# Four gate blocks in the opening of a hybrid layer, paired modulation visits, and ten early z blocks

## The chip, the cores and the metric

The kernel runs on one core of a Trainium2 chip. Its time is the device time of one execution in microseconds (us); the number given for a version is the median of its runs. The core's engines each work through their own list of instructions and meet at semaphores: PE (TensorE, matmuls; PEld is its weight loads, which overlap), DVE (VectorE), ACT (ScalarE), POOL (GpSimd) and SP (SyncE, which here issues nearly all DMA transfers). Results of PE go to banks of the PSUM memory (`pm`, `ps`), which the other engines read and free.

## The reference

One inference step of one decoder layer for a prompt of 256 tokens and 8 sequences with 8 new tokens each (320 rows), width 2048. Two branches read the same modulated input through one combined projection, and are merged by sigmoid gates:

```python
mod = silu(c) @ w_ada + b_ada                       # 9 conditioning rows (1 prompt, 8 sequences)
shift, scale, gate = split(mod, 3)
h = rms_norm(x, pre_norm_g) * (1 + scale) + shift
(a_qkv, a_z, a_b, a_a, b_q, b_k, b_v, b_z, i_q, i_k, i_w, g_a, g_b) = split_columns(h @ w_in)
y_a, s_new, conv_new = gdn_branch(...)              # short conv, gated delta rule, rms_norm(o) * silu(a_z)
y_b = attend(q, k, v, qi, i_w, i_k) * silu(b_z)     # top-k indexer, sparse attention
merged = sigmoid(g_a) * (y_a @ w_pa) + sigmoid(g_b) * (y_b @ w_pb)
return x + gate * rms_norm(merged @ w_out, post_norm_g)
```

The delta rule keeps a state S of 128 x 128 per head (32 heads, 8 sequences and the prompt) and updates it chunk by chunk: `s = s * g_tail + k_tail.T @ u`.

## The kernel before, in words

**Main products.** A product with a big weight matrix is done in float32 precision by splitting the weights (`whi`, `wlo`) and the activations (`xh`, `xl`) in a high and a low part. The unit of work is a half block: 8 x 128 rows of the weights by 128 columns, loaded by SP into `raw` (512 KB), split by ACT (`whi`) and DVE (`wlo = raw - whi`), and multiplied on PE by 8 x 3 matmuls with all 320 rows moving (`xh,whi`, `xl,whi`, `xh,wlo`). Two halves make a block of 128 output columns. `stream()` runs through a list of such half blocks, splits two ahead, and lets the other work ("sides", Python generators such as `prompt_chain`, `sample_chain`, `gate_gen`) put its instructions between them; a planner with its own clock decides when each side may go on. When something must be complete at a point (a buffer, a group), `force` puts all that is missing there in one go. The outcome is a fixed order for each engine.

**Stages.** *Opening* (`startup`): the modulation of x. In eight visits q, 256 columns of `shift` and 256 of `scale` are computed. `w_ada` comes in tiles of 1024 x 256 (`raw`, `rawx`, 1 MB); PE takes the 9 conditioning rows (padded to 32 columns, `cT`) as weights in four column groups of 32, each group summing every fourth row block, with 256 columns moving; `columns(q, e, h)` is one tile (e: shift or scale, h: half of the rows), `operands` copies the result to `msb`, adds the four partial sums and turns the rows into columns by four small products with `sel`, and modulates two row blocks of x into `xh`, `xl`. Each visit then has the two row blocks it needs to do, for its eighth of the width, part of the products of 8 index-query blocks (`iq_job`, 256 of the 320 rows), one value block (`bv_job`) and five auxiliary blocks (`held_job`, weights `awr` split to `awh`, `awl`). Partial sums of the first two are added in SBUF by DVE. These jobs wait in a list (`jobs`), and `run(n)` takes the next n. SP loads in the order in which `seq` lists: four tiles of `w_ada`, `i` (1 MB), `w` (720 KB), next visit; a load whose buffer is not free holds up those behind it.

*Attention*: the stream of the remaining 8 index-query blocks, 16 q, 16 z of mixer B, 16 blocks of the gate g_a (`ga`, kept in DRAM as `d_siga`), and the z blocks of mixer A named in `EARLY_Z` (two per entry); beside it all of the indexer, top-k and attention, and `gate_gen`, which computes the third part of the modulation like the opening does, in eight visits. *Gdn*: eight groups of four heads, each k, q, z and v blocks; beside it the recurrences. In a recurrence, PE multiplies the state (`w`, `S`) with `kq`, DVE forms `vt`, PE multiplies `XT,vt`, DVE and ACT form new `w`, PE multiplies `w,ktok`, and DVE updates S in 16 steps (`S<-S,gtr,ps`). z blocks that attention has done are left out of their groups, so groups 0 and 1 have 20 half blocks and the others 24. *Tail*: gate g_b, the two projections and the output product.

All engine calls go through one helper, so most rows of the profile carry its line, 63 (64 in the changed kernel), and are told apart by tile names.

Of the kernel before, what the change touches and what calls it, by code (L numbers as in the profile page):

```python
# [17 lines left out]
NP = 256  # L18
# [17 lines left out]
EARLY = 8  # L36
AHEAD = 4

EARLY_Z = (0, 4)
# [165 lines left out]
class Kernel:  # L205
# [259 lines left out]
    def consts(self):  # L465
# [6 lines left out]
        self.ident_b = self.l0.tile([128, 128], BF, name="ident_b")  # L472
        v.tensor_copy(self.ident_b, self.ident)
# [19 lines left out]
    def startup(self):  # L493
# [12 lines left out]
        awl = sp.tile([128, 2, 720], F32R, name="awl")  # L506
        seq = []
        for q in range(8):
            seq += [("a", q, 0), ("a", q, 1), ("a", 8 + q, 0), ("a", 8 + q, 1), ("i", q, 0), ("w", q, 0)]
        raws, aws, iqs = {}, {}, {}  # L510
        pos = {"n": 0}

        def load():
            while pos["n"] < len(seq):
                kind, q, h = seq[pos["n"]]
                r = awr if kind == "w" else ring
# [8 lines left out]
                elif kind == "w":  # L525
                    for d0, c0, n in ((0, C_IK, 144), (144, C_BA, 64), (208, C_BK, 512)):
                        nc.sync.dma_start(t[:, :, d0:d0 + n], w[rows, c0:c0 + n].rearrange("(k p) c -> p k c", p=128))
                    aws[q] = t
                else:
# [15 lines left out]
        for e in range(2):  # L545
            nc.scalar.dma_start(x[2][64 * e:64 * e + 64], xs[:, 1024 * e:1024 * e + 1024])
# [21 lines left out]
        seli = sp.tile([128, 9, 4], I32, name="seli")  # L568
        nc.gpsimd.iota(seli, pattern=[[-1, 9], [-32, 4]], base=0, channel_multiplier=1)
        self4 = sp.tile([128, 9, 4], F32, name="self4")  # L570
        nc.vector.tensor_scalar(self4, seli, 0.0, None, op0=OP.is_equal)
        self.sel = self.l0.tile([128, 9], F32, name="sel")
        nc.vector.tensor_reduce(self.sel, self4, axis=AX.X, op=OP.add)
# [17 lines left out]
        both = sp.tile([128, 128], F32, name="both")  # L591
        for e in range(2):
            self.tt(both[:, 64 * e:64 * e + 64], self.ident[:, 0:64], self.ident[:, 64:128], OP.add)
# [23 lines left out]
        msb = sp.tile([128, 512], F32, name="msb")  # L617
# [14 lines left out]
        def split_i(q, g):  # L632
# [13 lines left out]
            low()  # L646

# [48 lines left out]

        def first_jobs():
# [8 lines left out]
        def jobs(q):  # L706
            if q == 0:
                fifo.append(first_jobs)
            for h in range(3 if q == 0 else 0, EARLY):
                fifo.append(lambda h=h: iq_job(q, h))  # L710
            fifo.append(lambda: bv_job(q))
            for j in range(len(held)):
                fifo.append(lambda j=j: held_job(q, j))
# [5 lines left out]
        def columns(q, e, h, p):  # L719
            t, whole = raws.pop((q + 8 * e, h))  # L720
            for k in range(8):
                kb, j = 8 * h + k, k % 4
                self.mm(p[32 * j:32 * j + 32, 256 * e:256 * e + 256], self.cT[:, kb, :], t[:, k, :], start=(kb < 4),
                        stop=(kb >= 12), skip=True)
            drop(t, whole)

        def operands(q, turned=None):
# [3 lines left out]
            for e in range(4):  # L731
                self.mm(p[:, 9 * e:9 * e + 9], msb[:, 128 * e:128 * e + 128], self.sel)
# [3 lines left out]
            for e, qq in enumerate((q, 8 + q)):  # L736
                self.tt(mod[:, 2 * qq:2 * qq + 2, :], p[:, 18 * e:18 * e + 18].rearrange("p (e s) -> p e s", s=9),
# [11 lines left out]
        for q in range(8):  # L749
# [12 lines left out]
            else:  # L762
                idle_turns(10)
            if q == 1:
                run(2)
                split(0)
                run(2)
            p = self.ps_main.get()
            columns(q, 0, 0, p)
            if q == 0:  # L770
                idle_turns(14)
            columns(q, 0, 1, p)
            if q == 0:
                idle_turns(14)
            elif q == 1:
                run(4)
            else:
                split(q - 1)
                run(5)
            if q >= AHEAD:  # L780
                split_i(q, 0)
            columns(q, 1, 0, p)
            if q == 0:
# [5 lines left out]
                idle_turns(8)  # L789
            columns(q, 1, 1, p)  # L790
            self.act(msb, p)
# [4 lines left out]
            elif q > 1:  # L796
                run(4)
# [11 lines left out]
        run(5)  # L809
# [1637 lines left out]
```

## Time and profile before

| | |
|---|---|
| median of 3 runs | 2132.27 us (2132.07 to 2133.04) |
| profiled execution | 2132.65 us, span 2130.9 us |
| granted clock, mean | 0.998 |
| PE, PEld, DVE, ACT, POOL busy | 99%, 94%, 66%, 46%, 22% |
| opening, until the first half block of the stream | 0 to 169.5 us |
| attention | 169.5 to 715.7 us |
| gdn | 715.7 to 1659.5 us |
| tail | to the end |

Times in rows are in us from the start of the span; "mean ns" is the duration of one instruction, which for matmuls overlaps with the next: the cost of one on PE is the distance between starts. A matmul of two float32 operands is recorded as two passes. In brackets stands idle time of the engine ahead of a row, and what ended it.

### The profile page before, as it was taken

To read this page: it belongs to the slowest core of one execution; us is meant where nothing else is said; L and a number is where in the kernel's file an instruction comes from. 1 tells how busy PE (TensorE), PEld (TensorE's weight loads), DVE (VectorE), ACT (ScalarE), POOL (GpSimd) and SP (SyncE) were. 2 spreads that over 40 slices of the span, in tenths; PEclk is the share of its full clock that TensorE was granted. 3 is DMA by queue.
4 is the path that set the end of the run, shared out by engine and by line. 5 is a ranking of instruction groups with operands and counts; after the bars stand their busy time and mean duration, and the time that the engine had idled before them with its cause. 6 is when DMAs were issued, how large, how long until landed. Compare 5 with 4: busy or idle time off the path is not lost.

```text
span 2130.9 us, 43963 instructions
## 1 busy us (share of the span) xinstructions
PE 2099.3 (99%) x17055; PEld 2006.3 (94%) x17055; DVE 1410.9 (66%) x2881; ACT 989.6 (46%) x2257; POOL 463.1 (22%) x653
## 2 busy tenths in 40 slices
PE   7999999999999999999999999999999999999997
PEld 5889999899999999999999999999999999999997
DVE  4665657899755678868787878787746545445543
ACT  3235464333344455565656565656535424233343
POOL 2000100000001036545444444445440000000000
PEclk9999999999999999999999999999999999999999
DMA  9996656985787766777877777777787967555562
GB/s 332 355 309 173 181 151 178 289 256 151 201 238 239 205 181 173 211 210 207 207 200 199 208 196 210 193 212 192 200 218 210 268 180 218 161 155 146 166 178 85
DMA packets 720336, 438.91 MB, mean 206 GB/s; under 512 B 74144, under 2 KB 705536, under 8 KB 717824
## 3 DMA queue, kind: packets, MB, share of 16 engines
q1 hardware_dynamic: 716032, 413.45, 68.9%
q0 software_dynamic: 3616, 21.02, 3.0%
q8 instruction: 134, 2.20, 0.4%
q10 hardware_dynamic: 480, 1.65, 0.3%
q14 instruction: 74, 0.61, 0.1%
HBM read 386.81 MB, written 48.94 MB: 204 GB/s over the span
## 4 chain that ended last, share of the span: by engine, by line
PE 72%; issue 23%; DMA 2%; DVE 2%; ACT 0%; SPq 0%; DVEq 0%; POOL 0%; POOLq 0%; ACTq 0%
PE pm L63 56%; PE ps L63 16%; DMA raw<-in_w_ada_dram 1%; DVE S L63 1%; DMA rawx<-in_w_in_dram 1%; DVE wlo L63 0%; SPq L63 0%; DMA c<-in_c_sample_dram 0%; DVE awl L63 0%; DMA out_dram<-S 0%; ACT whi L63 0%; ACT ot L63 0%; DVE sga L63 0%; DVE w L63 0%; DVEq L2443 0%
## 5 line engine op out<-in xcount | busy, mean ns | idle before, releaser
L63 PE MATMUL pm<-xh,whi 128*128 128x320 f32 (+1 forms) x3284 | 996.1, 317 | 1.9 <-DVE qiS L63 0.8
L63 PE MATMUL pm<-xl,whi 128*128 128x320 f32 (+1 forms) x3284 | 962.1, 307 | 0.4 <-DVE xl L63 0.3
L63 DVE TENSOR_TENSOR wlo<-raw,whi 128x1024 fp32r<-128x1024 f32 x474 | 589.1, 1252 | 280.8 <-ACT whi L63 264.9
L63 PEld LDWEIGHTS pm<-xh,whi 128*128 128x128 f32 x3284 | 617.6, 188 | 32.2 <-issue 23.9
L63 PEld LDWEIGHTS pm<-xl,whi 128*128 128x128 f32 x3284 | 618.1, 188 | 1.7 <-DVE xl L63 0.8
L63 ACT ACTIVATE whi<-raw 128x1024 fp32r<-128x1024 f32 x474 | 497.7, 1058 | 169.7 <-PE pm L63 150.8
L63 PE MATMUL pm<-xh,wlo 128*128 128x320 f32 (+1 forms) x3284 | 547.6, 307 | 0.0
L63 PEld LDWEIGHTS pm<-xh,wlo 128*128 128x128 f32 x3284 | 495.4, 188 | 0.0
L63 POOL TENSOR_TENSOR X<-X,tmpx 48x31 f32<-48x31 f32 (+15 forms) x248 | 175.9, 709 | 19.4
L63 POOL TENSOR_TENSOR tmpx<-blk,X 48x31 f32<-48x31 f32 (+15 forms) x248 | 160.4, 647 | 51.0 <-DMA blk<-d_b 32.8
L63 PE MATMUL pm<-y1h,whi 128*128 128x320 f32 x512 | 151.3, 308 | 1.1 <-ACT y1h L63 1.1
L63 PE MATMUL pm<-y1l,whi 128*128 128x320 f32 x512 | 151.3, 307 | 0.2
L63 DVE SCALAR_TENSOR_TENSOR ps<-xp,cs,ps 128x344 f32<-128x344 f32 x192 | 111.5, 581 | 6.8
L63 POOL TENSOR_TENSOR rfin<-rfin,mh 128x3 f32<-128x3 f32 x1 | 0.8, 848 | 486.4 <-DVE rfin L63 486.4
L63 POOL TENSOR_TENSOR sc<-sc,mh 128x6 f32<-128x6 f32 (+1 forms) x24 | 43.6, 1815 | 277.0 <-DVE sc L63 213.0
L63 PEld LDWEIGHTS pm<-y1h,whi 128*128 128x128 f32 x512 | 95.7, 187 | 1.4 <-ACT y1h L63 1.3
L63 PEld LDWEIGHTS pm<-y1l,whi 128*128 128x128 f32 x512 | 96.1, 188 | 0.7 <-DVE y1l L63 0.7
L63 PE MATMUL pm<-y1h,wlo 128*128 128x320 f32 x512 | 85.4, 308 | 0.0
L63 PEld LDWEIGHTS pm<-y1h,wlo 128*128 128x128 f32 x512 | 77.7, 187 | 0.0
L63 DVE SCALAR_TENSOR_TENSOR S<-S,gtr,ps 128x128 f32<-128x128 f32 x256 | 67.4, 341 | 0.1
L63 ACT ACTIVATE xp<-pm 128x256 f32<-128x256 f32 (+1 forms) x128 | 32.0, 304 | 69.9 <-PE pm L63 69.9
L63 ACT ACTIVATE ot<-ot,sc 128x128 f32<-128x128 f32 x96 | 29.9, 390 | 72.3 <-DVE sc L63 72.3
(374 smaller groups left out, 2308.0 us busy)
## 6 DMA issues: line engine op xcount, KB each, us to landing
raw<-in_w_in_dram SPq DMA_DIRECT2D x336, 512.0 KB
raw<-in_w_pa_dram SPq DMA_DIRECT2D x64, 512.0 KB
rawx<-in_w_ada_dram SPq DMA_DIRECT2D x18, 1024.0 KB
a<-in_w_ada_dram SPq DMA_DIRECT2D x16, 1024.0 KB
S<-in_state_gdn_dram SPq DMA_DIRECT2D x32, 512.0 KB
out_dram<-S SPq DMA_DIRECT2D x32, 512.0 KB
raw<-in_w_pb_dram SPq DMA_DIRECT2D x32, 512.0 KB
raw<-in_w_out_dram SPq DMA_DIRECT2D x32, 512.0 KB
```

What stands on the lines that cost most here:

```text
L63: made = fn(*args, **kw)
```

## The change

1. `GATED = 4`: the first four gate blocks leave attention's list and are done in the opening. Each visit loads 512 KB more (`gwr`, one buffer) and runs four more jobs of 6 matmuls (`ga_job`); `split_g` splits the weights with the `whi`, `wlo` buffers; DVE adds each visit's part in SBUF, and after the last visit the sigmoid is taken and stored.
2. Visits work on pairs: one call of `columns` takes a tile of shift and one of scale, and the four column groups hold four different 128-column pieces, each summed over all row blocks, so that one transpose of `msb` replaces the four `sel` products. Loads and the layout of the sample rows of x are reordered to fit. `gate_gen` does the same: three DVE steps follow one transpose where two followed two products.
3. The split of the auxiliary weights moves ahead of the visit's first columns, the gate split lies between the two column calls, and the numbers in `run` change.
4. `EARLY_Z` grows from two entries to five: six more z blocks are done in attention, and groups 2, 3 and 4 of gdn have 20 half blocks instead of 24.

```diff
+GATED = 4
...
-EARLY_Z = (0, 4)
+EARLY_Z = (0, 4, 8, 12, 16)
...
+        gwr = Ring([sp.tile([128, 2, 128 * GATED], F32, name="gwr")])
+        ga = [self.auxf[:, 0:NT], self.vtok.rearrange("p c d -> p (c d)")[:, 0:NT]]
+        ga += [sp.tile([128, NT], F32, name=f"ga{j}") for j in range(GATED - 2)]
...
         for q in range(8):
-            seq += [("a", q, 0), ("a", q, 1), ("a", 8 + q, 0), ("a", 8 + q, 1), ("i", q, 0), ("w", q, 0)]
-        raws, aws, iqs = {}, {}, {}
+            seq += [("a", q, 0), ("a", 8 + q, 0), ("a", q, 1), ("a", 8 + q, 1), ("i", q, 0), ("w", q, 0), ("g", q, 0)]
+        raws, aws, iqs, gws = {}, {}, {}, {}
...
-                r = awr if kind == "w" else ring
+                r = {"w": awr, "g": gwr}.get(kind, ring)
...
+                elif kind == "g":
+                    nc.sync.dma_start(t, w[rows, C_GA:C_GA + 128 * GATED].rearrange("(k p) c -> p k c", p=128))
+                    gws[q] = t
...
-        msb = sp.tile([128, 512], F32, name="msb")
+        msb = sp.tile([128, 128], F32, name="msb")
...
+        def split_g(q):
+            r = gws.pop(q)
+            hi, lo = self.whi.get(), self.wlo.get()
+            hv, lv = (x.rearrange("p k c -> p (k c)").rearrange("p (k c) -> p k c", k=2) for x in (hi, lo))
+            halves[q, 2] = hi, lo, hv, lv
+            self.act(hv[:, :, :128 * GATED], r)
+            self.tt(lv[:, :, :128 * GATED], r, hv[:, :, :128 * GATED], OP.subtract)
+            gwr.put(r)
+            load()
...
+        def ga_job(q, j):
+            hi, lo, hv, lv = halves[q, 2]
+            p = self.ps_main.get()
+            products(q, p[:, :NT], hv, lv, 128 * j, 128, True, True)
+            add_to(q, p, [(ga[j], p[:, :NT])])
+            if j == GATED - 1:
+                self.whi.put(hi)
+                self.wlo.put(lo)
+                del halves[q, 2]
+            if q == 7:
+                t = ga[j]
+                self.act(t, t, AF.Tanh, scale=0.5)
+                self.ts(t, t, 0.5, 0.5, OP.mult, OP.add)
+                nc.sync.dma_start(self.d_siga[j], t)
...
+            for j in range(GATED):
+                fifo.append(lambda j=j: ga_job(q, j))
...
-        def columns(q, e, h, p):
-            t, whole = raws.pop((q + 8 * e, h))
+        def columns(q, h, p):
+            pair = [raws.pop((q + 8 * e, h)) for e in range(2)]
...
-                kb, j = 8 * h + k, k % 4
-                self.mm(p[32 * j:32 * j + 32, 256 * e:256 * e + 256], self.cT[:, kb, :], t[:, k, :], start=(kb < 4),
-                        stop=(kb >= 12), skip=True)
-            drop(t, whole)
+                kb = 8 * h + k
+                for j in range(4):
+                    f = 128 * (j % 2)
+                    self.mm(p[32 * j:32 * j + 32, 0:128], self.cT[:, kb, :], pair[j // 2][0][:, k, f:f + 128],
+                            start=(kb == 0), stop=(kb == KB - 1), skip=True)
+            for t in pair:
+                drop(*t)
...
         def operands(q, turned=None):
...
-            for e in range(4):
-                self.mm(p[:, 9 * e:9 * e + 9], msb[:, 128 * e:128 * e + 128], self.sel)
+            self.tr(p[:, 0:128], msb)
...
-                self.tt(mod[:, 2 * qq:2 * qq + 2, :], p[:, 18 * e:18 * e + 18].rearrange("p (e s) -> p e s", s=9),
+                self.tt(mod[:, 2 * qq:2 * qq + 2, :],
+                        p[:, 64 * e:64 * e + 64].rearrange("p (e s) -> p e s", s=32)[:, :, 0:9],
...
-                idle_turns(10)
+                idle_turns(34)
...
-                run(2)
+                run(5)
...
-                run(2)
+            elif q > 1:
+                run(3)
+                split(q - 1)
...
-            columns(q, 0, 0, p)
-            if q == 0:
-                idle_turns(14)
-            columns(q, 0, 1, p)
-            if q == 0:
-                idle_turns(14)
-            elif q == 1:
-                run(4)
-            else:
-                split(q - 1)
-                run(5)
-            if q >= AHEAD:
-                split_i(q, 0)
-            columns(q, 1, 0, p)
+            columns(q, 0, p)
...
-                idle_turns(8)
-            columns(q, 1, 1, p)
-            self.act(msb, p)
+                idle_turns(14)
+            else:
+                if q == 1:
+                    split_g(0)
+                    run(3)
+                else:
+                    run(3)
+                    split_g(q - 1)
+                    run(2)
+            if q >= AHEAD:
+                split_i(q, 0)
+            columns(q, 1, p)
+            self.act(msb, p[:, 0:128])
...
-            elif q > 1:
-                run(4)
+            else:
+                run(3 if q == 1 else 5)
...
-        run(5)
+        run(4)
...
+        split_g(7)
+        run(3)
...
-        run(3)
+        run(2)
...
-        run(2)
+        run(5)
...
-            yield self.ready(*pend)
+            yield self.ready(*pend) + 3.0
...
-            for k in range(KB):
-                j = k % 4
-                self.mm(p[32 * j:32 * j + 32, 0:256], self.cT[:, k, :], pend[k // 8][:, 256 * (k % 8):256 * (k % 8) + 256],
-                        start=(k < 4), stop=(k >= 12), skip=True)
+            for k in range(8):
+                for j in range(4):
+                    kb = 2 * k + j // 2
+                    c0 = 256 * (kb % 8) + 128 * (j % 2)
+                    self.mm(p[32 * j:32 * j + 32, 0:128], self.cT[:, kb, :], pend[kb // 8][:, c0:c0 + 128],
+                            start=(k == 0), stop=(k == 7), skip=True)
...
-            self.act(m[:, 0:256], p[:, 0:256])
+            self.act(m[:, 0:128], p[:, 0:128])
...
-            for e in range(2):
-                self.mm(p[:, 9 * e:9 * e + 9], m[:, 128 * e:128 * e + 128], self.sel)
-            for e in range(2):
-                k = 2 * q + e
-                self.ts(self.gatp[:, k, :], p[:, 9 * e:9 * e + 9], self.feat[:, 32 + k:33 + k], self.feat[:, 64 + k:65 + k],
-                        OP.add, OP.mult)
+            self.tr(p[:, 0:128], m[:, 0:128])
+            g = self.gatp[:, 2 * q:2 * q + 2, :]
+            part = lambda c: p[:, c:c + 64].rearrange("p (e s) -> p e s", s=32)[:, :, 0:9]
+            each = lambda c: self.feat[:, c + 2 * q:c + 2 * q + 2].rearrange("p (e o) -> p e o", o=1).to_broadcast(
+                [128, 2, 9])
+            self.tt(g, part(0), each(32), OP.add)
+            self.tt(g, part(64), g, OP.add)
+            self.tt(g, g, each(64), OP.mult)
...
+                        lambda p, h: self.gate_done(p, GATED + h, self.d_siga, self.t_r), r)
```

**Where the order changes.** PE in the first visit, from the last columns to the first products. Before (`raw`, `cT`: columns; `ident`: fillers that keep PE busy):

```order
L63 MATMUL ps_67<-ident 128x128 x8
L63 MATMUL pm_65<-raw_75,cT 32x256 x8
L63 MATMUL ps_67<-ident 128x128 x5
L63 MATMUL pm_65<-sel,msb 128x9 x4
L63 MATMUL ps_67<-ident 128x128 x18
L63 MATMUL pm_65<-xh,whi_78 128x256
```

After:

```order
L64 MATMUL pm_65<-rawx_163,cT 32x128 x2
L64 MATMUL pm_65<-raw_75,cT 32x128 x2
L64 MATMUL ps_67<-ident 128x128 x5
L64 MATMUL pm_65<-ident,msb 128x128
L64 MATMUL ps_67<-ident 128x128 x18
L64 MATMUL pm_65<-xh,whi_78 128x256
```

The columns are rows of 128 that alternate between two tiles, and one transpose stands where the four sel products stood.

SP in the opening, the loads of the first visit and the start of the second, after the change:

```order
L64 DMA raw_76<-in_w_in_dram 128x2x1024
L64 DMA awr_164<-in_w_in_dram 128x2x144
L64 DMA awr_164<-in_w_in_dram 128x2x64
L64 DMA awr_164<-in_w_in_dram 128x2x512
L64 DMA gwr<-in_w_in_dram 128x2x512
L64 DMA raw_77<-in_w_ada_dram 128x8x256
```

The gate weights stand behind the auxiliary ones and ahead of the next visit's tiles; before, `raw_77<-in_w_ada_dram` followed the auxiliary weights directly.

PE in gdn, the end of the eight `w,ktok` products whose results DVE adds to S, and what follows. Before, in the third group (`ps_70` and so on are PSUM banks):

```order
L63 MATMUL ps_68<-w_7351,ktok_7327 128x256
L63 MATMUL ps_67<-w_7351,ktok_7327 128x256
L63 MATMUL ps_70<-w_7351,ktok_7327 128x256
L63 MATMUL ps_72<-w_7351,ktok_7327 128x256
L63 MATMUL pm_65<-xh,whi_78 128x320
L63 MATMUL pm_65<-xl,whi_78 128x320
```

After, at the last half block of the third group:

```order
L64 MATMUL ps_70<-w_8087,ktok_8063 128x256
L64 MATMUL ps_72<-w_8087,ktok_8063 128x256
L64 MATMUL ps_69<-w_8087,ktok_8063 128x256
L64 MATMUL ps_67<-w_8087,ktok_8063 128x256
L64 MATMUL ps_68<-w_8089,kq_8056 128x256 x2
L64 MATMUL ps_70<-vt_8085,XT_8081 128x128 x2
L64 MATMUL ps_72<-vt_8084,XT_8081 128x128 x2
L64 MATMUL ps_69<-vt_8085,XT_8081 128x128 x2
L64 MATMUL ps_67<-w_8090,ktok_8064 128x256
```

Before, main products follow at once. After, the second chain's `kq`, three `XT` products and its eight `w,ktok` follow with no main product among them; the next one stands 17 rows further on, behind these and six transposes. The same run stands at the end of the groups after it, 3 and 4.

DVE beside it, before (`wlo` rows are weight splits for the stream):

```order
L63 SCALAR_TENSOR_TENSOR S_7359<-S_7359,gtr,ps_68 128x128 x4
L63 SCALAR_TENSOR_TENSOR S_7359<-S_7359,gtr,ps_67 128x128 x4
L63 SCALAR_TENSOR_TENSOR S_7359<-S_7359,gtr,ps_70 128x128 x4
L63 SCALAR_TENSOR_TENSOR S_7359<-S_7359,gtr,ps_72 128x128 x4
L63 COPY ct_7316<-xp_7312 128x27
L63 TENSOR_SCALAR ps_69<-xp_7312,cs_101 128x344
L63 SCALAR_TENSOR_TENSOR ps_69<-xp_7312,cs_101,ps_69 128x344 x3
L63 TENSOR_SCALAR w_7352<-ps_71,sc_7362 128x128 x2
L63 TENSOR_SCALAR w_7354<-ps_67,sc_7362 128x128 x2
L63 TENSOR_TENSOR wlo_81<-raw_77,whi_78 128x1024
L63 SCALAR_TENSOR_TENSOR vt_7349<-ps_70,neG,vt_7349 128x128 x2
```

After:

```order
L64 SCALAR_TENSOR_TENSOR S_8095<-S_8095,gtr,ps_70 128x128 x4
L64 SCALAR_TENSOR_TENSOR S_8095<-S_8095,gtr,ps_72 128x128 x4
L64 SCALAR_TENSOR_TENSOR S_8095<-S_8095,gtr,ps_69 128x128 x4
L64 SCALAR_TENSOR_TENSOR S_8095<-S_8095,gtr,ps_67 128x128 x4
L64 SCALAR_TENSOR_TENSOR vt_8085<-ps_68,neG,vt_8085 128x128 x2
L64 TENSOR_SCALAR w_8090<-ps_70,sc_8098 128x128 x2
L64 TENSOR_SCALAR w_8088<-ps_72,sc_8098 128x128 x2
L64 TENSOR_SCALAR w_8091<-ps_69,sc_8098 128x128 x2
```

The `vt_8085` of the second chain stands directly behind the 16 S updates of the first, and the `w` steps for both chains and 16 more updates follow it; before, the conv work of the stream, a `wlo` split and other steps lay between.

More of the change, by code (lines that the diff above doesn't have):

```diff
@@ L471, in consts @@
         v.tensor_scalar(self.ident, ji, 0.0, None, op0=OP.is_equal)
-        self.ident_b = self.l0.tile([128, 128], BF, name="ident_b")
-        v.tensor_copy(self.ident_b, self.ident)
         self.ones = self.l0.tile([128, 128], F32, name="ones")
@@ L544, in startup @@
         xs = i["x_sample"].rearrange("b t d -> (b t) d")
-        for e in range(2):
-            nc.scalar.dma_start(x[2][64 * e:64 * e + 64], xs[:, 1024 * e:1024 * e + 1024])
+        nc.scalar.dma_start(x[2], xs.rearrange("r (e c) -> (r e) c", e=2))
         nc.scalar.dma_start(x[1], i["x_prompt"][0, 128:256, :])
@@ L566, in startup @@
         self.ps_main.put(p)
[L568 to L573, printed above, removed]
         ssq = sp.tile([128, 3], F32, name="ssq")
@@ L591, in startup @@
         both = sp.tile([128, 128], F32, name="both")
+        pairs = lambda t: t.rearrange("p (r e) -> p r e", e=2)
         for e in range(2):
-            self.tt(both[:, 64 * e:64 * e + 64], self.ident[:, 0:64], self.ident[:, 64:128], OP.add)
+            self.tt(pairs(both)[:, :, e], pairs(self.ident)[:, :, 0], pairs(self.ident)[:, :, 1], OP.add)
         def norm(t):
@@ L864, in gate_gen @@
             p = self.psum()
-            for e in range(2):
-                self.mm(p[:, 9 * e:9 * e + 9], m[:, 128 * e:128 * e + 128], self.sel)
-            for e in range(2):
-                k = 2 * q + e
-                self.ts(self.gatp[:, k, :], p[:, 9 * e:9 * e + 9], self.feat[:, 32 + k:33 + k], self.feat[:, 64 + k:65 + k],
-                        OP.add, OP.mult)
+            self.tr(p[:, 0:128], m[:, 0:128])
[6 more added lines that the diff above has]
+            self.tt(g, g, each(64), OP.mult)
             self.ps_side.put(p)
@@ L913, in modulate @@
         hs = h[:, NP:NT].rearrange("p (b t) -> p b t", t=TS)
-        c0 = NP + 64 * (k // 8)
         bc = lambda a: a[:, k, 1:9].rearrange("p (b o) -> p b o", o=1).to_broadcast([128, NB, TS])
-        self.tt(hs, p[:, c0:c0 + 64].rearrange("p (b t) -> p b t", t=TS), bc(gs), OP.mult)
+        self.tt(hs, p[:, NP:384].rearrange("p (b t e) -> p e b t", t=TS, e=2)[:, k // 8], bc(gs), OP.mult)
         self.tt(hs, hs, bc(mod), OP.add)
@@ L1008, in attn_chunks @@
         chunks += self.pairs(w, C_BZ, 16, self.bz_done, r)
-        ga = self.pairs(w, C_GA, 16, lambda p, h: self.gate_done(p, h, self.d_siga, self.t_r), r)
+        ga = self.pairs(w, C_GA + 128 * GATED, 16 - GATED,
+                        lambda p, h: self.gate_done(p, GATED + h, self.d_siga, self.t_r), r)
         ga[0].before = lambda: self.spawn(self.conv_gen(0))
```

## The prediction

> **What bounds the kernel now.** I read the page first, then a table of stretches, then the opening and one busy place of the gdn stage row by row.
>
> ```profile
> span 2130.9 us, 43963 instructions
> PE 2099.3 (99%) x17055; PEld 2006.3 (94%) x17055; DVE 1410.9 (66%) x2881; ACT 989.6 (46%) x2257; POOL 463.1 (22%) x653
> ```
>
> PE is busy nearly all the time, so a change pays by the PE work it removes and costs by the waits it makes. The stretches (columns: length, then busy time and count of PE, PEld, DVE, ACT, POOL, the granted clock, DMA share, GB/s) are, in order, the opening after its first 30 us, the second gdn group, and one full gdn group (the fourth).
>
> ```profile
> 30.00:169.50 139.50, 133.68 (x1222) 113.72 (x1221) 89.22 (x240) 43.23 (x61) 6.31 (x7) 1.00 1.00 322
> 790.70:882.70 92.00, 90.88 (x761) 86.39 (x759) 72.62 (x163) 47.29 (x125) 53.66 (x76) 1.00 0.67 173
> 991.40:1098.40 107.00, 107.00 (x877) 102.91 (x877) 82.95 (x198) 62.32 (x175) 51.56 (x71) 1.00 0.75 203
> ```
>
> The clock is full, so it is no term. Only in the opening is the DMA share 1.00. The second group, with 20 half blocks instead of 24, already runs in 92.0 us: DVE is 79% busy there, 78% in the full group.
>
> **The yardstick** is a half block of main products: 24 matmuls, of which these rows give the starts of two in a row.
>
> ```profile
> 831.73 0.31 PE L63 MATMUL pm<-xh,whi 128*128 128x320 f32 x1
> ...
> 835.25 0.31 PE L63 MATMUL pm<-xh,whi 128*128 128x320 f32 x1
> ```
>
> That is 3.52 us, or 0.147 us a matmul. A full group is then 24 x 3.52 = 84.5 us of main products and 22.5 us of side work; the second group 70.4 and 21.6.
>
> **Part 1, four gate blocks into the opening.** One late visit of the opening reads:
>
> ```profile
> 133.87 0.49 PE L63 MATMUL ps<-ident,x 128*128 128x128 f32 x3
> 134.20 0.49 PE L63 MATMUL pm<-ident,x 128*128 128x128 f32 x3
> 134.62 1.06 PE L63 MATMUL pm<-sel,msb 128*128 128x9 f32 x8
> 135.53 0.35 PE L63 MATMUL ps<-xh,awh 128*80 128x320 f32 x1
> ...
> 140.05 1.07 PE L63 MATMUL pm<-raw,cT 128*32 128x256 f32 x16
> 140.94 1.05 PE L63 MATMUL pm<-rawx,cT 128*32 128x256 f32 x16
> 141.92 0.39 PE L63 MATMUL ps<-xh,whi 128*128 128x256 f32 x1
> ...
> 146.00 1.93 PE L63 MATMUL pm<-rawx,cT 128*32 128x256 f32 x32
> 147.87 0.39 PE L63 MATMUL pm<-xh,whi 128*128 128x256 f32 x1
> ...
> 150.99 0.49 PE L63 MATMUL ps<-ident,x 128*128 128x128 f32 x3
> ```
>
> A visit is 150.99 - 133.87 = 17.1 us and nearly all PE work. The change adds 24 matmuls of 320 to each of eight visits: 192 x 0.147 = +28.2 us on the path, since PE is the path. What it takes from DMA is bounded by two rows: 512 KB more on the 5.7 MB that a visit now loads in 17.1 us gives 18.6 us at the present pace, and 20.2 us at the mean 322 GB/s of the stretch. PE's visit becomes 17.1 + 3.5 - 0.8 = 19.8 us (the 0.8 comes in part 2), so PE should lead after the first two or three visits. The new load has a single buffer and stands on SP's queue ahead of the next visit's loads, so it can hold them up. It is freed by the split about 7.5 us into a visit (columns 1.9, three jobs 2.7, the split itself some 2.3 by the 1.22 us of a DVE split plus ACT's half), and the four loads behind it need 12.5 us more, so they land as the next visit starts. That covers it with almost nothing to spare. DVE gets 1.22 + 4 x 0.49 = 3.2 us more a visit and goes from 64% (89.2 of 139.5) to about 71%, still beside PE:
>
> ```profile
> L63 DVE TENSOR_TENSOR wlo<-raw,whi 128x1024 fp32r<-128x1024 f32 x12 | 14.4, 1222 | 5.5 <-ACT whi L63 5.5
> L63 DVE TENSOR_TENSOR bvT<-pm,bvT 128x320 f32<-128x320 f32 x5 | 2.5, 492 | 1.8 <-PE pm L63 1.8
> ```
>
> **Part 2, paired visits and one turn.** The eight sel rows take 135.53 - 134.62 = 0.91 us; one transpose like the three of x that take 134.20 - 133.87 = 0.33 is 0.11, with a start of its own 0.12. Eight visits: -6.3 us. The columns change from 16 passes of 256, four at a time, to 64 passes of 128. The same shape is not in the trace. Upper bound: `a,a` below has two column groups side by side, 15.7 us / 128 pairs = 0.123 us a round, so 16 rounds are 1.96 us. Lower bound: today's first 16 passes, which the next call follows after 0.89 us (140.05 to 140.94), twice: 1.78. Now 32 passes take 1.87 (146.00 to 147.87), between the two. I take 1.87, no change; the ends are -1.4 and +1.5 us over 16 calls.
>
> ```profile
> L63 PE MATMUL ps<-a,a 128*64 128x128 f32 x256 | 15.7, 276 | 0.0
> L63 PE MATMUL ps<-a,qS 32*64 32x256 f32 x512 | 15.9, 380 | 0.0
> L63 PE MATMUL ps<-XT,blk 32*32 32x32 f32 x320 | 5.8, 194 | 0.0
> L63 PE MATMUL ps<-a,cT 128*32 128x256 f32 x256 | 15.5, 382 | 0.0
> L63 PE MATMUL ps<-sel,s 128*128 128x9 f32 x32 | 4.0, 236 | 0.0
> ```
>
> [...]
>
> In attention the gate visits lose three of four sel passes, 8 x 0.33 = -2.6 us. The longer pass list and the three small DVE steps hide behind main products; uncovered, 24 DVE steps at the 0.26 us that an S update takes below would cost 6 us.
>
> The first visit must wait for two loads where one did, and does 32 passes after the last one where it did 16: +0.9 us. Three waits of today's later visits come from late loads, 2.85 us together (the third through a late split). With 3.5 us more of PE work a visit they should mostly go; the first visits stay paced by DMA, so I credit 2.3.
>
> ```profile
> 49.95 1.07 PE L63 MATMUL pm<-raw,cT 128*32 128x256 f32 x16 [0.36 <-DMA raw<-in_w_ada_dram]
> 52.86 0.85 PE L63 MATMUL pm<-raw,cT 128*32 128x256 f32 x12 [1.84 <-DMA raw<-in_w_ada_dram]
> ...
> 97.31 0.39 PE L63 MATMUL pm<-xh,whi 128*128 128x256 f32 x1 [0.65 <-ACT msb L63]
> ```
>
> **Part 3, the later split and the run counts** have the same work in another place. In the last visit the gate split now stands on DVE behind the auxiliary split and the additions, with four iq jobs and bv, 3.7 us of PE work, as cover: +0.5 us at the end of the opening, 0 to 2. The opening so gives 28.2 - 6.3 + 0.9 - 2.3 + 0.5 = **+21 us** (18 to 24), and the stream should start near 190 instead of 169.5.
>
> **Part 4, six z blocks into attention.** Attention loses four gate blocks and gains six z blocks: 2 x 2 x 3.52 = +14.1; with the gate visits' -2.6 and about 0.9 of stall that longer cover hides, **+10.6 us**. Groups 2, 3 and 4 of gdn lose four half blocks each: 12 x 3.52 = **-42.2 us**. The side work of those groups stays, with less to cover it. The order shows where that bites: at the last half block of each of the three groups, two recurrence chains stand on PE in one run with no main product between. Today the same work is spread:
>
> ```profile
> 966.21 1.02 PE L63 MATMUL ps<-w,kq 128*128 128x256 f32 x4
> 967.16 1.15 PE L63 MATMUL ps<-w,ktok 32*128 32x256 f32 x16
> 968.24 0.41 PE L63 MATMUL pm<-xh,whi 128*128 128x320 f32 x1
> 968.49 0.31 PE L63 MATMUL pm<-xl,whi 128*128 128x320 f32 x1
> ...
> 970.10 0.60 PE L63 MATMUL ps<-vt,XT 128*128 128x128 f32 x4
> 970.54 0.60 PE L63 MATMUL ps<-w,ktok 128*128 128x256 f32 x2
> 970.98 0.61 PE L63 MATMUL ps<-vt,PT 128*128 128x128 f32 x4
> ```
> ```profile
> 967.92 0.61 DVE L63 SCALAR_TENSOR_TENSOR vt<-ps,neG,vt 128x128 f32<-128x128 f32 x2 [1.10 <-ACT ot L63]
> 968.45 3.69 DVE L63 SCALAR_TENSOR_TENSOR S<-S,gtr,ps 128x128 f32<-128x128 f32 x14
> ```
>
> The run's PE work by these rows and their neighbours: kq 0.95 twice, ktok 1.08 twice, eight products of 0.44 (three vt,XT, two w,ktok x2, two vt,PT, one kq,kq) and six transposes of 0.1, 8.2 us in all. But DVE has 16 S updates of 0.26 us twice in it, and the second chain's vt step stands behind the first 16. I follow it: kq ends at 0.95, vt at 2.2 (it starts 0.76 after its matmuls), S until 6.4, the other vt 6.9; PE, idle since 3.0, resumes at 7.0; three w steps by ACT and DVE until 9.0 to 9.9; second S until 13.0 to 14.1; the transposes that need its banks end at 13.4 to 14.6. So 5.1 to 6.4 us of PE wait per run. Where such a run of half the length stands today, PE waits like this:
>
> ```profile
> 880.01 0.71 PE L63 MATMUL ps<-kq 128*128 128x128 f32 x4
> 881.25 0.44 PE L63 MATMUL ps<-ident,vf 128*128 128x128 f32 x2 [0.53 <-DVE S L63]
> 882.28 0.66 PE L63 MATMUL ps<-ident,vf 128*128 128x128 f32 x4 [0.60 <-DVE S L63]
> 882.69 0.39 PE L63 MATMUL pm<-xh,whi 128*128 128x320 f32 x1
> ```
>
> From 880.01 to 882.69 PE does 1.1 us of work, so one chain's 16 updates cost about 1.6 us, two would cost 3.2 without the vt step. The spread order pays something that the run does not: the first main matmul after side work takes 0.25 instead of 0.15 us (968.24 to 968.49), about nine times, 0.9 us. I take 5.7 - 0.9 = 4.8 per run: **+14.4 us** (7 to 18). DVE work is not the kernel's bound, but here it is the only cover gone. Behind the run stands DVE's next weight split, with two finished half blocks (7 us) ahead of it: enough, barely.
>
> **Sum:** 21.0 + 10.6 - 42.2 + 14.4 = +3.8 us on a profiled execution of 2132.65 us (span 2130.9), which lies 0.4 above the median 2132.27. I forecast **2136 us**. A difference under 0.2%, 4.3 us, can hardly be told from none, and this one is just under.
>
> **Rivals.**
> *The runs cost nothing.* If the vt step and S do not hold PE, because other PE work fits between or DVE is ahead, the 14.4 falls to 0 to 4 and the result is -11 to -7: about 2124. For it: the second group runs today with 20 half blocks in 92.0 us and only 1.1 us of listed S waits. Against it: that group has half the run. The sign turns where a run costs 3.5 us.
> *Transfers or the single buffer lead the opening.* At 20.2 us a visit the opening grows by another 0.4 x 7 = 3 us, and if the new load's turn-around shows by half a us a visit, 4 more: about 2143. For it: DMA share 1.00 throughout. Against: PE's visit grows by more than DMA's.
> *DVE's splits come late after the runs.* Two splits of 1.2 us plus the 2.7 us of chain work behind them delay the next half blocks by 3 us a run: about 2145. Against: DVE has a fifth of its time free.
> [...]
>
> **How the numbers follow.** Forecast 0.56, from 2131 to 2141: 0.34 of it within 0.2%, 0.22 slower. Runs at no cost 0.21, of which 0.19 is faster. Opening led by transfers 0.12 and late splits 0.08, both slower. 62 ns 0.03, slower. So faster 0.19, same 0.36, slower 0.45. The range 2126 to 2144 leaves out most of the 62 ns case and the outer halves of the first and the third.
>
> **What would show it.** Visits of 19.7 to 20 us with no sel rows and one ident,msb row of 0.12; columns of 1.8 to 2.0 us; main stream from about 190; gdn groups 2 to 4 near 97 us each; and in the list of waits PE behind DVE S, or behind vt, of 12 us or more instead of 1.1. If those groups take 92 us, the first rival holds; if visits are over 20.5 us with waits for gwr or columns, the second. I would be most wrong if the S chain overlaps in a way that the order hides.

## The result and the profile after

The changed kernel takes 2147.86 us (median of 4 runs, 2146.32 to 2147.97) against 2132.47 us for the kernel before in the same comparison: ratio 1.007, 95% interval 1.0053 to 1.0088. It is 15.4 us slower, where 2136 us (2126 to 2144) was forecast. The profiled execution took 2147.89 us, 15.2 us more than that of before.

The first lines of its page:

```profile
span 2146.2 us, 45362 instructions
PE 2105.2 (98%) x17745; PEld 2024.5 (94%) x17745; DVE 1427.1 (66%) x2914; ACT 989.1 (46%) x2261; POOL 444.9 (21%) x652
```

PE has 6 us more busy time, the rest is waiting. A table of stretches (length, busy time and count of PE, PEld, DVE, ACT, POOL, granted clock, DMA share, GB/s) shows the opening after 30 us, attention, and gdn's groups 1 to 7, counted from 0 as in the prediction:

```profile
30.00:188.10 158.10, 154.98 (x1805) 146.20 (x1804) 107.79 (x272) 48.12 (x70) 7.57 (x7) 1.00 0.94 304
188.10:746.70 558.60, 557.92 (x5275) 529.62 (x5274) 387.25 (x700) 244.44 (x514) 29.31 (x43) 1.00 0.71 206
821.60:913.60 92.00, 90.88 (x760) 86.40 (x758) 71.03 (x163) 47.25 (x125) 53.09 (x76) 1.00 0.67 173
913.60:1014.90 101.30, 98.86 (x792) 93.22 (x791) 78.33 (x202) 57.32 (x168) 47.45 (x71) 0.97 0.76 199
1014.90:1117.10 102.20, 98.34 (x783) 92.03 (x782) 78.49 (x194) 57.02 (x166) 49.17 (x76) 0.97 0.71 192
1117.10:1216.30 99.20, 94.67 (x778) 88.63 (x776) 76.28 (x187) 56.63 (x166) 46.36 (x70) 1.00 0.72 189
1216.30:1326.90 110.60, 109.19 (x886) 104.02 (x884) 84.48 (x198) 65.52 (x189) 53.91 (x77) 1.00 0.73 198
1326.90:1438.20 111.30, 108.18 (x880) 103.34 (x880) 85.30 (x211) 66.17 (x192) 35.47 (x53) 1.00 0.75 198
1438.20:1542.40 104.20, 104.20 (x849) 100.75 (x848) 78.98 (x169) 57.57 (x151) 57.10 (x78) 1.00 0.74 198
```

Group 1 is as short as before, at 92.0 us. Groups 2 to 4, short for the first time, take 101.3, 102.2 and 99.2 us, and 5 and 6, which have not been touched, take 110.6 and 111.3 instead of 107.1. Stage by stage, from the start of the first half block in each (main products are 3.52 us a half block, 72 before and 60 after):

| | before | after | difference | forecast |
|---|---|---|---|---|
| opening | 169.5 | 188.1 | +18.6 | +21.0 |
| attention | 546.2 | 558.6 | +12.4 | +10.6 |
| main products of groups 2 to 4 | 253.4 | 211.2 | -42.2 | -42.2 |
| the rest of groups 2 to 4 | 69.4 | 91.5 | +22.2 | +14.4 |
| groups 5 to 7 | 321.4 | 326.2 | +4.8 | 0 |
| groups 0, 1 and tail | | | -0.4 | 0 |

PE's waits, with how often and the longest, show who is late:

```profile
PE pm L64 <- ACT whi L64: 4.6, 4, 1.7
PE ps L64 <- DVE vt L64: 4.4, 5, 1.6
PE pm L64 <- DVE wlo L64: 3.5, 8, 1.1
PE ps L64 <- DVE S L64: 3.0, 7, 0.6
```

Before, these lines summed to 1.4 us. And the run at the end of group 2, on PE:

```profile
999.91 1.02 PE L64 MATMUL ps<-w,kq 128*128 128x256 f32 x4
1000.87 1.15 PE L64 MATMUL ps<-w,ktok 32*128 32x256 f32 x16
1002.39 1.10 PE L64 MATMUL ps<-w,kq 128*128 128x256 f32 x4 [0.38 <-DVE vt L64]
1003.33 0.71 PE L64 MATMUL ps<-vt,XT 128*128 128x128 f32 x4
1004.36 0.71 PE L64 MATMUL ps<-vt,XT 128*128 128x128 f32 x4 [0.32 <-DVE S L64]
1006.69 0.75 PE L64 MATMUL ps<-vt,XT 128*128 128x128 f32 x4 [1.62 <-DVE vt L64]
1007.46 3.74 PE L64 MATMUL ps<-w,ktok 32*128 32x256 f32 x18
1010.99 1.06 PE L64 MATMUL ps<-vt,PT 128*128 128x128 f32 x4
...
1014.92 0.39 PE L64 MATMUL pm<-xh,whi 128*128 128x320 f32 x1
```

It lasts 999.91 to 1014.92, 15.0 us. Up to 1007 it goes as the prediction followed it: the second chain's XT product waits for the vt step that stands behind 16 S updates. But then the 16 `w,ktok` passes, 1.1 us elsewhere, and the two passes behind them take 3.5 us, and four `vt,PT` passes take 0.85 us instead of 0.44. No wait is listed there. The clock says why:

```profile
1003.30:1006.70 3.40, 1.46 (x10) 1.06 (x9) 3.40 (x14) 1.56 (x5) 1.53 (x6) 1.00 0.08 31
1006.70:1010.00 3.30, 3.27 (x21) 2.32 (x21) 2.26 (x9) 0.62 (x2) 2.79 (x7) 0.61 0.85 252
1010.00:1014.90 4.90, 4.90 (x23) 4.54 (x23) 4.90 (x20) 0.00 (x0) 4.31 (x8) 0.56 0.65 185
```

After a stretch of 3.4 us in which PE worked for 1.46 us, the granted clock fell to half. Cut finer, the same view gives 0.50 from 1007.46 to 1014.28, 6.8 us of the run, and 1.00 on both sides. Group 3 ends in the same run, 15.2 us long, with 0.50 from 1109.86 to 1116.68. Group 4's run, 13.0 us, has the products of the two chains in another order than the section on the change says, and the clock stays at 1.00 there.

### The profile page after: what moved, and what is told of

The parts are those of the page before. It is cut to its first block, busy times and chain, and to the rows that moved or that the text cites. A ratio compares the mean times of both kernels' runs of the same rounds, so it can differ in the third digit from the quotient of the medians.

```text
span 2146.2 us, 45362 instructions
## 1 busy us (share of the span) xinstructions
PE 2105.2 (98%) x17745; PEld 2024.5 (94%) x17745; DVE 1427.1 (66%) x2914; ACT 989.1 (46%) x2261; POOL 444.9 (21%) x652
## 4 chain that ended last, share of the span: by engine, by line
PE 66%; issue 23%; DVE 6%; ACT 2%; DMA 2%; SPq 0%; DVEq 0%; POOL 0%; POOLq 0%; ACTq 0%
PE pm L64 50%; PE ps L64 16%; DVE wlo L64 2%; DVE S L64 1%; DVE ps L64 1%; ACT ot L64 1%; DMA rawx<-in_w_ada_dram 1%; ACT whi L64 0%; DMA out_dram<-s 0%; SPq L64 0%; ACT ps L64 0%; DMA c<-in_c_sample_dram 0%; ACT gbt L64 0%; DMA d_ya<-zf 0%; DMA zf<-d_z 0%
## 5 line engine op out<-in xcount | busy, mean ns | idle before, releaser
L64 ACT ACTIVATE whi<-raw 128x1024 fp32r<-128x1024 f32 x466 | 488.3, 1057 | 172.3 <-PE pm L64 148.1
L64 POOL TENSOR_TENSOR tmpx<-blk,X 48x31 f32<-48x31 f32 (+15 forms) x248 | 155.8, 628 | 130.8 <-DMA blk<-d_b 113.1
L64 POOL TENSOR_TENSOR X<-X,tmpx 48x31 f32<-48x31 f32 (+15 forms) x248 | 171.5, 692 | 19.4
L64 POOL TENSOR_TENSOR sc<-sc,mh 128x6 f32<-128x6 f32 (+1 forms) x24 | 37.7, 1573 | 215.2 <-DVE sc L64 215.2
L64 ACT ACTIVATE vt<-ps,sc 128x128 f32<-128x128 f32 (+1 forms) x112 | 39.1, 409 | 55.2 <-PE ps L64 55.1
```

The source lines that it names most:

```text
L64: made = fn(*args, **kw)
```

## The experiments

**The paired visits alone.** Before with the paired visits and the later split, no gate blocks in the opening, and `EARLY_Z` as before. Against the changed kernel:

```diff
-GATED = 4
-EARLY_Z = (0, 4, 8, 12, 16)
+GATED = 0
+EARLY_Z = (0, 4)
...
-            seq += [..., ("w", q, 0), ("g", q, 0)]
+            seq += [..., ("w", q, 0)]
...
```

> Paired visits, one turn and the later split alone: no gate blocks in the opening, EARLY_Z as before. From attention on the order is that of the kernel before except for the gate visits. Theory (the pairs gain what their rows say, the loss lies in the z blocks): opening 8 x 0.8 = 6 us shorter less about 1 for the first visit, gate visits 2 to 3 us shorter, so 2123 to 2127 us. Rival 1 (the opening is held by DMA anyway, so the saved PE time turns into waits for loads): only the gate visits' part shows, 2129 to 2131 us. Rival 2 (the columns of 128 cost more than before in place): 2132 us or more.

Measured: 2126.11 us, ratio 0.9964 (0.995 to 0.9978), 7 us faster than before. The opening is 165.3 us, 4.2 shorter where some 5 were expected, and attention 543.7, 2.5 shorter. The opening gives part of the saved PE time back: between 30 us and its end PE sits idle for 7.8 us instead of 5.8, behind loads and behind DVE's `qiS`. The theory holds. The columns of 128 cost no more: in the changed kernel the passes start in rounds of four every 0.11 us, and 64 passes take 1.88 us, where the row for 32 passes of 256 gave 1.87.

**The z blocks put back.** The changed kernel with four gate blocks in the opening, and:

```diff
-EARLY_Z = (0, 4, 8, 12, 16)
+EARLY_Z = (0, 4)
```

> The changed kernel with EARLY_Z back at two entries: attention has 56 blocks instead of 62, and groups 2 to 4 of gdn have 24 half blocks again. Work is the same, only its place differs. Theory (the six z blocks cost 27 us of waits in gdn: 22 in groups 2 to 4, 5 in groups 5 to 7): gdn 943 to 945 us as before, attention 516 us plus 0 to 12 us for side work that 56 blocks cannot cover; 2120 to 2132 us. Rival (the z move costs nothing, the loss comes from gate blocks that no longer cover attention's side work): 2147 us or more, with the loss in attention.

Measured: 2139.86 us, ratio 1.0029 (1.0018 to 1.0039). gdn is back at what it was (groups 2 to 7 at 109.0, 107.1, 107.1, 107.1, 107.1, 107.2 us), as the theory says, but attention takes 533.3 us, not 516 to 528. Its last half block has 31.6 us of side work and waits behind it: the sample attention, which 56 blocks do not cover. For 10.2 us of that half block the granted clock is 0.50. The chain of PE there (rows with waits of 1 us and more):

```profile
693.12 2.31 PE L64 MATMUL ps<-a,a 128*64 128x128 f32 x32 [1.92 <-ACT t L64]
701.88 0.92 PE L64 MATMUL ps<-ident,a 32*128 32x32 f32 x33 [3.68 <-ACT a L64]
705.10 4.02 PE L64 MATMUL ps<-a,a 128*64 128x128 f32 x32 [2.29 <-issue]
715.98 0.99 PE L64 MATMUL ps<-ident,a 32*128 32x32 f32 x33 [3.75 <-ACT a L64]
```

Both sides were partly right: the z move costs 27 us in gdn, and without it the gate move costs some 18 us in attention (533.3 less 112 x 3.52 leaves 139.1 us beside main products, against 121.3 with the paired visits alone).

**The z blocks alone.** Before, and nothing else than:

```diff
-EARLY_Z = (0, 4)
+EARLY_Z = (0, 4, 8, 12, 16)
```

> The kernel before with EARLY_Z of five entries and nothing else: attention 66 blocks, groups 2 to 4 short. Work is unchanged. Theory: the waits in gdn come with the short groups whatever the opening does: 25 to 30 us more than before, 2157 to 2162 us, with runs of both chains at the end of groups 2 to 4. Rival (the runs need the gate move too, by the planner's timing): within 10 us of before, 2132 to 2142 us.

Measured: 2196.44 us, ratio 1.0295 (1.0278 to 1.0313): 63 us slower, more than twice what the theory gave. Groups 1 to 6 take 95.4, 107.2, 121.6, 97.8, 119.9 and 110.7 us. Two runs are much longer here, 46.6 us with the last half block of group 3 and 29.2 with that of group 5. Beside longer waits for `whi`, the list of PE's waits has one for `X` that the changed kernel's list does not have:

```profile
PE pm L63 <- ACT whi L63: 11.5, 8, 4.3
PE ps L63 <- DMA X<-d_x: 10.6, 2, 6.6
```

`d_x` carries the triangular inverse that POOL computes for each group. Both waits for it stand in the run of group 3, so there the order has fallen behind by that step too; in the run of group 5 PE does not wait for it. The clock has a larger part here than in the changed kernel: it is 0.50 for 27.3 us of the first run, 10.2 us of the second, and 10.2 us elsewhere in gdn.

**Short S updates.** The changed kernel, every instruction in the same place, but S updates on 8 columns; the rest of S is left as loaded:

```diff
-    self.stt(S[:, bb, v, :], S[:, bb, v, :], g, ps[j][:, c:c + 128], OP.mult, OP.add)
+    ve.engine.scalar_tensor_tensor(S[:, bb, v, 0:8], S[:, bb, v, 0:8], g, ps[j][:, c:c + 8], op0=OP.mult, op1=OP.add)
```

(`g`, `c` and `ve` stand for the row factor, the column and DVE; the planner is told of the long update, so that its order stays.)

> The changed kernel in exactly its order of instructions, but each of the S updates on DVE takes 8 of its 128 columns (the rest of S is left as loaded). Theory (PE waits in the runs for DVE's 32 updates of 0.26 us): an update takes about 0.1 us, a run shrinks from 15.0 to 10 or 11 us, and the later groups lose their 5 us too: 2128 to 2136 us, PE's waits behind DVE S and vt nearly gone. Rival (PE waits for the chain of hand-overs between PE, ACT and DVE, not for DVE's time): 2143 to 2148 us.

Measured: 2132.24 us, ratio to before 0.9996 (0.9986 to 1.0005): 15.6 us less than the changed kernel. The run at the end of group 2:

```profile
998.32 1.02 PE L64 MATMUL ps<-w,kq 128*128 128x256 f32 x4
...
1003.09 0.75 PE L64 MATMUL ps<-vt,XT 128*128 128x128 f32 x4 [0.31 <-DVE vt L64]
1003.87 2.27 PE L64 MATMUL ps<-w,ktok 32*128 32x256 f32 x18
...
1007.74 0.82 PE L64 MATMUL ps<-ident,vf 128*128 128x128 f32 x6
```

It lasts from 998.32 to 1008.32, 10.0 us, and the 18 passes take 2.1 us again. Groups 2 to 4 are 96.2, 96.8 and 96.6 us: 13.1 of their 22.2 us have gone. Groups 5 to 7 keep 3.1 of 4.8. An update takes 0.14 us (256 in 35.5 us) instead of 0.26. DVE's time in S is the larger part, as the theory says, with the clock inside it, and not all.

**Four entries, in a row and spread.** The changed kernel with one entry fewer, and with four that leave groups between them:

```diff
-EARLY_Z = (0, 4, 8, 12, 16)
+EARLY_Z = (0, 4, 8, 12)
```
```diff
-EARLY_Z = (0, 4, 8, 12, 16)
+EARLY_Z = (0, 4, 20, 28)
```

> The changed kernel with EARLY_Z of four entries (0, 4, 8, 12): attention 60 blocks, as many as before; groups 2 and 3 of gdn short, 4 full. Theory (each consecutive short group ends in a run of both chains): runs at the end of groups 2 and 3, each some 7 to 9 us above the side work of before, 3 to 5 us more in the groups after them, attention as covered as before: 2138 to 2142 us. Rival (the loss is in the third run and what follows it): 2131 to 2135 us.

> The same with EARLY_Z of (0, 4, 20, 28): as many blocks as with (0, 4, 8, 12) in attention, but the short groups are 0, 1, 5 and 7, with full groups ahead of 5 and 7. Theory (a chain falls behind only where short groups follow one another; a full group lets it catch up): shorter runs at the end of 5 and 7, together 6 to 10 us above before: 2126 to 2131 us. Rival (a short group costs the same wherever it stands): 2138 to 2142 us, as with (0, 4, 8, 12).

Measured: 2146.9 us, ratio 1.0068 (1.0051 to 1.0085), in a row; 2139.86 us, 1.0032 (1.0019 to 1.0045), spread. In a row there are runs at the end of groups 2 and 3 (99.6 and 102.0 us), as expected, but the groups after them lose more, with 109.8, 111.3, 105.9 and 112.0 us: 10.6 above before where 3 to 5 were expected. A third short group hardly adds to that. Spread, the time lies in the rival's range and not in the theory's. In gdn the theory holds: groups 2 to 4 are as before, 5 takes 93.9 and 7 takes 98.2, together 5.9 us above two full groups less four half blocks each, a little under the 6 to 10 expected. The rest was lost elsewhere: the projection behind the last recurrence waits for its input (the profile is of the longest run, 2142.2 us):

```profile
1663.09 0.41 PE L64 MATMUL pm<-y1h,whi 128*128 128x320 f32 x1 [1.37 <-ACT y1h L64]
1666.36 0.63 PE L64 MATMUL pm<-y1h,whi 128*128 128x320 f32 x1 [1.90 <-ACT y1h L64]
1671.53 0.64 PE L64 MATMUL pm<-y1h,whi 128*128 128x320 f32 x1 [2.83 <-ACT y1h L64]
1674.82 0.63 PE L64 MATMUL pm<-y1h,whi 128*128 128x320 f32 x1 [1.59 <-ACT y1h L64]
```

The stretch from the end of group 7 takes 11.5 us more than before (one half block 15.2 instead of 3.5). These waits are 7.7 us, and the granted clock is 0.50 from 1664.42 to 1678.07. A short last group alone does not bring this: the next kernel has one too, and there the stretch is as long as before. What does was not found out.

**Two gate blocks.** The changed kernel with two gate blocks in the opening and one z entry beside the two of before, so that attention has 60 blocks as before:

```diff
-GATED = 4
+GATED = 2
...
-EARLY_Z = (0, 4, 8, 12, 16)
+EARLY_Z = (0, 4, 28)
...
-                    run(2)
+                    run(1)
...
-                run(3 if q == 1 else 5)
+                run(3 if q == 1 else 4)
```

> Paired visits with two gate blocks in the opening instead of four, and EARLY_Z of (0, 4, 28): attention has 60 blocks as before, and only the last group of gdn is short besides 0 and 1. Theory (each gate block in the opening gains about 1.3 us where it fills waits, and a last short group costs 3 to 6 us of run): 2125 to 2128 us, within 2 us of the paired visits alone. Rival (no run costs anything in the last group, since the tail covers it): 2121 to 2124 us, the fastest of all.

Measured: 2124.42 us, ratio 0.9963 (0.9949 to 0.9977), just under the expected range. The opening is 174.8 us: two gate blocks, 14.1 us of products, lengthen it by 9.4. Four lengthen it by 22.8 for 28.2. So the opening had some 5 us of room, and the first two blocks fill most of it. The short last group costs 1.9 us, and attention is as covered as before. It is the fastest measured, but its interval overlaps that of the paired visits alone.

**The norm's small product on POOL.** In the changed kernel's groups 5 and 6, PE waits for weight splits. One of these waits, on POOL, DVE and ACT:

```profile
1323.56 1.32 POOL L64 TENSOR_TENSOR sc<-sc,mh 128x6 f32<-128x6 f32 x1 [4.21 <-DVE sc L64]
```
```profile
1325.85 4.21 DVE L64 SCALAR_TENSOR_TENSOR S<-S,gtr,ps 128x128 f32<-128x128 f32 x16
...
1330.68 1.81 DVE L64 SCALAR_TENSOR_TENSOR ps<-xp,cs,ps 128x344 f32<-128x344 f32 x3
1332.40 0.49 DVE L64 TENSOR_TENSOR sc<-sc,sc 128x6 f32<-128x6 f32 x1
```
```profile
1332.93 1.86 ACT L64 ACTIVATE ot<-ot,sc 128x128 f32<-128x128 f32 x6 [5.25 <-DVE sc L64]
1334.70 1.99 ACT L64 ACTIVATE whi<-raw 128x1024 fp32r<-128x1024 f32 x2
```

POOL has finished at 1324.9, but DVE's product of 6 columns stands behind 16 S updates and the conv until 1332.4. ACT waits for it with the weight splits behind, and PE waits 1.72 us for `whi` at 1335.79. So, with nothing else moved:

```diff
     self.tt(m[:, 12:18], m[:, 6:12], self.mh.to_broadcast([128, 6]), OP.pow, eng=nc.gpsimd)
+    nc.gpsimd.engine.tensor_tensor(mv(12), mv(12), qf, OP.mult)
     yield
-    self.tt(mv(12), mv(12), qf, OP.mult)
...
```

(The planner is told of the product at its old place on DVE, so that its order stays.)

> The changed kernel in its order, but the small product of the head norm (sc times the row factor) is done by POOL right after its power, not by DVE, where it stands behind 16 S updates and conv steps. In the changed kernel's sixth and seventh group ACT waits for it with the weight splits behind, and PE then for whi (4.6 us in all) and wlo (3.5). Theory (part of what groups 5 to 7 lose is this hand-over): PE's waits behind whi fall to about 1 us, groups 5 and 6 are 1 to 4 us shorter together: 2143 to 2146 us. Rival (the splits are late for ACT's own load or for the raw buffers): no change, 2147 to 2148.5 us.

> The kernel with paired visits, two gate blocks in the opening and EARLY_Z of (0, 4, 28), with the same product on POOL. Theory: in full groups nothing waited for it (PE's waits behind whi are 1.5 us in all), so at most 1 us is won: 2123 to 2125 us. Rival (every group loses a little by it): 2119 to 2122 us.

Measured: the changed kernel falls to 2134.97 us, ratio to before 1.0011 (1.0002 to 1.002), 12.9 us less, where 2 to 5 were expected; in the kernel with two gate blocks nothing changes (2124.91 us, 0.9962, 0.9948 to 0.9976). The waits for `whi` are gone from the list. Groups 2 to 4 are 99.5, 99.4 and 96.8 us (7.1 less), 5 and 6 are 108.2 and 107.4 (6.3 less). Not all of the 7.1 is this wait: the half blocks with the runs of groups 2 and 3 took 1.5 and 0.5 us less, because the clock stayed at 1.00 in the first and was 0.50 for 3.4 us instead of 6.8 in the second, although PE waited as long in them. Why the clock fell less there is not shown. The rows of group 2's run:

```profile
1002.60:1006.00 3.40, 1.46 (x10) 1.05 (x9) 3.40 (x14) 1.56 (x5) 1.76 (x6) 1.00 0.06 22
1006.00:1009.30 3.30, 3.27 (x26) 2.44 (x27) 3.09 (x12) 0.63 (x2) 2.76 (x7) 1.00 0.85 251
```

The stretch has the same 1.46 us of PE work as that in the changed kernel, and no fall behind it.

**Fillers in the runs.** The changed kernel with ten transposes ahead of each XT product of a prompt chain in a run, 60 in all (`forcing` is set where the rest of a chain is run off at a half block's end):

```diff
+        if self.forcing:
+            for _ in range(10):
+                nc.tensor.engine.transpose(p[:, 0:128], self.ident, self.ident)
```

> The changed kernel with ten idle transposes (0.11 us each, results overwritten) ahead of each of the two XT products of the prompt chains in each of the three runs: 60 in all, put where PE waits anyway. Theory (in the run PE is so idle that the granted clock falls to 0.56 behind the wait, which costs 1.5 to 3 us in a run where it happens): the clock stays 1.00 in the runs, groups 2 and 3 are 1 to 2.5 us shorter: 2143 to 2147 us. Rival (the clock falls by something else, or the fillers only add their own 2.1 us a run): 2148 to 2154 us.

Measured: 2145.5 us (5 runs within 0.34 us), 2.4 less than the changed kernel; ratio to before 1.0057 (1.0044 to 1.0071). The stretches of group 2's run:

```profile
1004.00:1007.40 3.40, 3.40 (x37) 3.19 (x38) 3.13 (x13) 1.12 (x4) 2.77 (x9) 1.00 0.34 97
1007.40:1012.80 5.40, 4.48 (x36) 3.45 (x29) 5.24 (x21) 0.13 (x1) 4.64 (x10) 1.00 0.86 241
```

The clock stays at 1.00, and the half blocks with the runs take 19.5, 19.5 and 19.6 us instead of 20.8, 21.0 and 19.6. The run of group 2 is 13.7 us long. Work added to a waiting PE made these half blocks shorter: the theory holds. The rows show it; the ratios to before of this kernel and the changed one have intervals that overlap.

**The z blocks alone with short S updates.** The kernel of the z blocks alone, with this beside it; the rest of S is left as loaded here too:

```diff
-    self.stt(S[:, bb, v, :], S[:, bb, v, :], g, ps[j][:, c:c + 128], OP.mult, OP.add)
+    ve.engine.scalar_tensor_tensor(S[:, bb, v, 0:8], S[:, bb, v, 0:8], g, ps[j][:, c:c + 8], op0=OP.mult, op1=OP.add)
```

> The kernel before with EARLY_Z of five entries, in the same order, with S updates of 8 columns instead of 128 (the rest of S as loaded). With full updates it took 2196 us. Theory (there too PE waits for DVE's updates, what stands behind them on DVE and ACT, and the clock that falls in the waits): more than half of the 63 us goes, 2145 to 2165 us. Rival (its two long runs wait for the triangular inverse on POOL and its transfers, which the updates do not touch): 2175 us or more.

Measured: 2177.61 us, ratio 1.0207 (1.0191 to 1.0222): 19 of 63 us go. PE still waits 10.7 us for `X<-d_x`, and the long runs are 41.4 and 24.2 us. The time lies in the rival's range, and the longer run does wait for the inverse. The other does not, and in the longer one the clock is 0.50 for 20.5 us; how much each costs was not told apart. Why that kernel falls behind by the inverse and the changed one does not, with the same short groups, was not found out.

## Why the prediction was wrong

It forecast +3.8 us on the profiled execution and +15.2 came. Each term of the sum went the way that was forecast. What failed is two terms that were put at nothing: the weight splits behind the runs, and the clock.

*Groups 2 to 4 beside their main products, +14.4 forecast, +22.2 measured.* The chain of the run was followed rightly, and "I take 5.7 - 0.9 = 4.8 per run" holds in both its parts. The runs take 15.0, 15.2 and 13.0 us. Less the forecast's 8.2 us of work each that is 18.6 us, and 15.7 without the 2.9 that the fillers took away in groups 2 and 3, against the 17.1 of three times 5.7. The credit for fewer switches came too: a main product follows side work 24 to 26 times in a full group and 16 to 18 times in a short one, and the time lost at these places fell by 2.5 us in the three groups, against 2.7. What the sum did not have is the clock and the half blocks outside the runs.

*The clock, 0 forecast, 2.9 measured.* "The clock is full, so it is no term" was read from the rows of before and carried over to runs in which PE mostly waits. At 0.50 for 6.8 us, two of the three runs are 1.4 and 1.6 us longer than with fillers.

*What stands behind the runs, 0 forecast, some 6 us in groups 2 to 4 and 4.8 in 5 to 7.* This is the step that cost most. The prediction named DVE's next split as "enough, barely" and left it at that, looking two half blocks ahead. The work that was late was another: the norm's product on DVE, ACT's scaling behind it, and the splits behind that, up to two groups later. Taking that one hand-over from DVE gave 12.9 us in all: 2.0 were the clock, 5.1 the half blocks outside the runs, and the rest the groups behind, which then take 319.8 us, 1.6 less than before. That is the third rival (late splits after the runs, 2145 us, 0.08), by a path through ACT that the prediction did not see.

Of the signs that it named, the columns (1.88 us) and the start of the stream (188.1 us) came. Groups 2 to 4 were to be near 97 us each and PE's listed waits behind S and `vt` 12 us or more; the groups are 101.3, 102.2 and 99.2 us, and the waits 7.4 us.

*The opening, +21.0 forecast, +18.6 measured.* Pairs and gates were priced apart, and 2.3 us of today's waits were credited. With the paired visits alone the opening falls by 4.2, and four gate blocks add 22.8 of 28.2 us: the waits that they fill are about 5 us. Visits are 20.3 us early and 19.9 later and bounded by PE as forecast (1.0 us of waits for `w_ada` after the first 30 us, none for `gwr`), so the second rival fell. The chance of 0.03 in the forecast is for a pass of 62 ns, which no run shows; the columns took 29 ns a pass (64 in 1.88 us).

*Attention, +10.6 forecast, +12.4 measured.* The two added blocks and the gate visits came as worked out (+14.1 - 2.5); the 0.9 us of hidden stall did not come, and 0.8 more stays unexplained.

The first rival, runs at no cost, is excluded by the rows of the run. Against before, the paired visits are worth 7 us, and the z blocks' 27 us of waits in gdn bury that and the opening's 5.

## What to carry to other kernels

When main products are taken from beside a recurrence, the recurrence's own latency appears on PE (15.7 us in the runs of groups 2 to 4, without the clock), and more of it where short stretches follow one another (14.1 us in two in a row, 5.9 in two spread); follow not only the engine that waits in the run, but what stands behind the run on each in-order engine, for two stages on. A product of a few columns between two engines may hold up the big splits behind it; do it on the engine that already has its input (12.9 us here). In a kernel whose splits have time to spare, as with two gate blocks, that gives nothing (2124.91 us against 2124.42). And price PE work that stands among waits for a clock that may be half: 0.50 for 6.8 us made two runs here 1.4 and 1.6 us longer than with fillers.

## What the runs showed of the hardware

The granted clock fell without a long gap. In the changed kernel it was 0.50 twice in gdn, for 6.82 us each (1007.46 to 1014.28 and 1109.86 to 1116.68). The 3.41 us just ahead of the two falls held 1.46 and 1.76 us of PE work, with a longest listed wait of 1.62 us.

As little PE work did not always bring a fall. With the norm's product on POOL, the run of group 2 has the same waits, and 1.46 us of PE work in 3.40 us (1002.60 to 1006.00), and the clock stayed at 1.00; in that kernel's group 3, where PE waited as long, it was 0.50 for 3.4 us. With fillers the 3.40 us around the wait held 3.40 us of PE work (1004.00 to 1007.40), and the clock stayed at 1.00 too. What decides where the clock falls was not shown.
